# A hybrid decoder block: the second branch's output projection in seven-product quads, halves at both ends, and a new list schedule

## The chip, the cores and the metric

The kernel runs on one core of a Trainium2 chip. The metric is the device time of one execution in microseconds (us); for the kernel before it is the median of three runs. TensorE does the matmuls (PE in the profile, with PEld for its weight loads), VectorE (DVE) and ScalarE (ACT) do the elementwise work, GpSimd (POOL) issues the DMAs that add into what they find, and SyncE (SP) issues the plain loads.

## The reference

One layer, sequence 512, width 1024, fp32; the feed-forward width is 2816 (5632 columns in `w_up`).

```python
h = rmsnorm(x);  p_a, p_b, q, p_g = split(h @ w_in)
gb, gc, v = split(p_a);  y_a = (gb * causal_conv3(gc * v)) @ w_a_out          # branch 0
u, ug = split(p_b)
y_b = silu(layernorm(causal_conv31(u * sigmoid(ug)) + bias)) @ w_b_out         # branch 1
k, vm = split(rmsnorm(mem) @ w_kv)                                             # 256 memory tokens
y_c = attention(q, k, vm, heads=4) @ w_att_out                                 # branch 2
g = sigmoid(p_g + b_gate)
x = x + (g[0] * y_a + g[1] * y_b + g[2] * y_c) @ w_o
gt, up = split(causal_conv3(rmsnorm(x) @ w_up))
x = x + (silu(gt) * up) @ w_down
return rmsnorm(x)
```

## The kernel before

**Precision.** Every operand of a large product is split in two: a high part (`whi`, a rounded copy that ScalarE makes, L444 for weights) and a low part (`wlo`, the difference, by VectorE, L448). A product is then three matmuls: high by high, high by low, low by high. A 128 x 1024 piece of weights that goes through this is a *unit* (`split_job`, `unit_job`); there are four buffers for split units (`UNIT_BUFS`), so the split of a unit can't begin before the unit four places earlier in TensorE's order has been used. With `lo_from` the low part takes another way: ScalarE writes minus the high part (`wn`) and a DMA of POOL's queue adds the weights to it.

**Quads.** The input projection and the up-projection take their 2 x 2 blocks of products with seven block products instead of eight (the Strassen and Winograd scheme). A *quad* covers 1024 rows by 512 columns of weights. `quad_loads` loads four blocks u, v, s, r by SP and makes the sums of weights s5, s6, s7, s3, by accumulating DMAs of POOL or partly by VectorE; seven units come of it, in the order 1, 2, 5, 6, 7, 4, 3 or one close to it. `multiply` (L624) runs one product: 24 matmuls of 256 columns. The other operand stands in seven *forms* with two parts each (`b00`, `b10`, `t5`, `t6`, `t7`, `b11`, `t4`; tiles `fb00h`, `fb00l` and so on), and the three banks a, b, c of a quad are read seven times (`quad_reads`: r1, r5, r6, r4 by ScalarE, r2, r7, r3 by VectorE). 18 quads make the input projection (names in `QUAD_ORDER`: `glu`, `q`, `gate` (branch, half), `cv`, `bb`), 11 the up-projection. `w_o` and the down-projection are seven-product sums too, on larger blocks: `w_o` in the order a, b, f, c, d, e, g, the down-projection as a, b, d, c, f and e, g.

**The branches' output projections.** Each of the three was 8 units of 24 matmuls of 512 columns (`merge_product`, L1349 to L1351): four pairs of output blocks `m`, two halves `g` of the rows. VectorE reads each bank with the branch's gate as a factor (`weigh`), adds branches 2 and 0 (`sum` 0), and adds branch 1 into the tiles `mg` that `w_o` takes as its left operand (`sum` 1). Branch 2's units run after the second gate quad of branch 2, branch 0's after its own gates; branch 1's stand last, directly ahead of `w_o`, as its operand is ready last: the layer norm's scale and `swish`, then a split into `ybh`, `ybl`. `w_o`'s f = m11 - m10 needs all of branch 1; a and b need its first token rows; c, d and e are differences that follow.

**Order.** TensorE's order is written out by hand: `pe()` appends to `seq`, and lists such as `beside` and `first` put other work between the quads' products. The other engines' jobs are placed by a list scheduler (`Jobs`): a job has an engine, an estimated duration, what it follows, buffers that it takes and uses. `latest_starts` works out when each is due at the latest for TensorE; of the jobs that could start next the one with the earliest start, and then the earliest due time, goes first. `LATER` shifts the due times of whole kinds of jobs, `AHEAD` says how far ahead of its due time a kind may start. The result is a fixed queue for each engine (`issue_in_program_order`); an engine waits at an instruction whose operand isn't there, whatever stands behind it. Within a tie the order is that of a Python set. The rows of the input for the residual are loaded late, after `late_rows`.

**The two ends.** At the start TensorE runs nine matmuls on the identity (`warm_up`, L1697), then the first key unit in two halves (`K0`, L818, L822), two value units V 0 0 and V 0 1 (L396), a key unit, another one, and then sums of squares of the memory (`msq`, L734) by a matmul with ones. At the end the down-projection's last sum g runs for row tile 0 and then, as `("pd", "g", "rest")`, 15 matmuls of 512 columns for row tile 1; VectorE adds the bank to the residual (`read`, L1977), ScalarE squares it with a running sum (L1982) and takes the root, VectorE scales the tile (`scaled`, L2004), and it is stored.

## Time and profile before

| | |
|---|---|
| Median of 3 runs | 931.41 us (930.99 to 931.84) |
| The profiled execution | 931.52 us, of it the span 929.3 us |
| TensorE's granted clock in it | 0.997 |
| Busy: TensorE, VectorE, ScalarE | 916.8, 837.3, 672.5 us |
| DMA | 190.59 MB, 205 GB/s on the mean |

The profile's page gives busy times by engine and a line of digits for each, in 40 slices of 23.2 us; the chain that ended last, followed back from the end; and groups of instructions by line and operands. The rows of the timeline that the prediction quotes have a start (us from the start of the span), a duration, the engine, the line, the operation, output and input tiles with their shapes, and how many instructions the row takes together; in brackets stands how long the engine had been idle before, and what released it. A wait that is given by its total names the waiting group, the one that released it, and then total us, times and the longest.

### The profile page before, as it was taken

Reading aid. Unit: us, or ns where it says so; the run is one execution under the profiler, and the core shown is the slowest. Engines: PE = TensorE matmul, PEld = TensorE weight load, DVE = VectorE, ACT = ScalarE, POOL = GpSimd, SP = SyncE. Lnnn points to the kernel's source line nnn. Section 1 sums busy time; section 2 is a strip of 40 time slices with the busy share of each in tenths; the row PEclk is TensorE's granted clock in tenths of the full one; section 3 lists DMA queues with packets and bytes.
Section 4 is the critical chain, followed back from the end, with each engine's and each line's share of the span. In section 5 each row is a group of like instructions: output and inputs, shape, how many; then the busy total and the mean of one; then the engine's idle time right before and its main releaser. Section 6 shows DMA issues by size and latency. Waiting matters only on the chain.

```text
span 929.3 us, 16689 instructions
## 1 busy us (share of the span) xinstructions
PE 916.8 (99%) x6644; PEld 860.5 (93%) x6644; DVE 837.3 (90%) x948; ACT 672.5 (72%) x908; POOL 126.5 (14%) x153
## 2 busy tenths in 40 slices
PE   8999999999999999999999999999999999999996
PEld 7999999999989999999899888898999999988885
DVE  6898999969889999999996778897899889999986
ACT  7676988759978879878856743766767676765655
POOL 0121111101111112110100011021211121002300
PEclk9999999999999999999999999999999999999998
DMA  9999678857676799967955598499999878779962
GB/s 356 371 269 236 137 171 178 201 133 136 170 185 170 177 191 243 210 174 183 226 115 158 186 314 179 97 246 295 258 226 235 209 141 166 195 268 329 251 125 91
DMA packets 54077, 190.59 MB, mean 205 GB/s; under 512 B 6128, under 2 KB 6256, under 8 KB 54000
## 3 DMA queue, kind: packets, MB, share of 16 engines
q0 software_dynamic: 20880, 75.24, 45.5%
q1 hardware_dynamic: 32400, 113.23, 34.0%
q8 instruction: 52, 0.85, 0.4%
q10 hardware_dynamic: 720, 1.06, 0.3%
q14 instruction: 25, 0.20, 0.1%
HBM read 185.31 MB, written 4.19 MB: 204 GB/s over the span
## 4 chain that ended last, share of the span: by engine, by line
PE 93%; DMA 3%; ACT 2%; DVE 1%; issue 1%; SPq 0%; ACTq 0%; POOLq 0%
PE bank L624 56%; PE bank L395 6%; PE bank L397 6%; PE bank L396 6%; PE bank L1349 5%; PE bank L1350 5%; PE bank L1351 5%; DMA wf<-in_w_up 2%; PE bank L871 2%; DMA mem<-in_mem_t 1%; ACT whi L444 0%; DVE wlo L448 0%; PE ss L750 0%; PE bank L1098 0%; ACT j L1982 0%
## 5 line engine op out<-in xcount | busy, mean ns | idle before, releaser
L444 ACT CAST whi<-wf 128x1024 fp32r<-128x1024 f32 (+1 forms) x195 | 202.9, 1044 | 100.9 <-PE bank L624 40.1
L448 DVE TENSOR_TENSOR wlo<-wf,whi 128x1024 fp32r<-128x1024 f32 (+1 forms) x189 | 228.3, 1214 | 29.8 <-ACT whi L444 29.4
L1170 ACT ACTIVATE tp<-u,pk 128x510 f32<-128x510 f32 (+22 forms) x184 | 119.7, 706 | 7.5 <-DVE acc L1177 6.5
L1177 DVE TENSOR_TENSOR acc<-acc,tp 128x1022 f32<-128x1022 f32 (+22 forms) x92 | 109.5, 1193 | 4.2 <-ACT tp L1170 2.4
L582 POOL DMA_DIRECT2D wf<-in_w_in x48 | 42.5, 894 | 229.7 <-DVE wlo L448 164.0
L624 PE MATMUL bank<-ft6h,wlo 128*128 128x256 f32 x232 | 64.4, 278 | 1.2 <-DVE wlo L448 1.2
L624 PE MATMUL bank<-ft6h,whi 128*128 128x256 f32 x232 | 64.6, 278 | 1.0 <-ACT gt L651 1.0
L624 PE MATMUL bank<-fb10h,whi 128*128 128x256 f32 x232 | 64.4, 278 | 0.0
L624 PE MATMUL bank<-fb00h,whi 128*128 128x256 f32 x232 | 64.4, 278 | 0.0
L624 PE MATMUL bank<-fb00l,whi 128*128 128x256 f32 x232 | 64.3, 277 | 0.0
L624 PE MATMUL bank<-fb00h,wlo 128*128 128x256 f32 x232 | 64.3, 277 | 0.0
L624 PE MATMUL bank<-ft7h,whi 128*128 128x256 f32 x232 | 64.3, 277 | 0.0
L624 PE MATMUL bank<-ft7l,whi 128*128 128x256 f32 x232 | 64.3, 277 | 0.0
L624 PE MATMUL bank<-ft7h,wlo 128*128 128x256 f32 x232 | 64.3, 277 | 0.0
L624 PE MATMUL bank<-fb11h,whi 128*128 128x256 f32 x232 | 64.3, 277 | 0.0
L624 PE MATMUL bank<-ft5h,wlo 128*128 128x256 f32 x232 | 64.2, 277 | 0.0
L624 PE MATMUL bank<-ft5h,whi 128*128 128x256 f32 x232 | 64.2, 277 | 0.0
L624 PE MATMUL bank<-ft5l,whi 128*128 128x256 f32 x232 | 64.2, 277 | 0.0
L624 PE MATMUL bank<-ft6l,whi 128*128 128x256 f32 x232 | 64.2, 277 | 0.0
L624 PE MATMUL bank<-fb10h,wlo 128*128 128x256 f32 x232 | 64.2, 277 | 0.0
L624 PE MATMUL bank<-fb10l,whi 128*128 128x256 f32 x232 | 64.2, 277 | 0.0
L624 PE MATMUL bank<-fb11l,whi 128*128 128x256 f32 x232 | 64.1, 276 | 0.0
(392 smaller groups left out, 3143.8 us busy)
## 6 DMA issues: line engine op xcount, KB each, us to landing
wf<-in_w_in SPq DMA_DIRECT2D x52, 512.0 KB, 4.9
wf<-in_w_in POOLq DMA_DIRECT2D x48, 512.0 KB, 5.8
wf<-in_w_up SPq DMA_DIRECT2D x29, 512.0 KB, 5.3
wf<-in_w_up POOLq DMA_DIRECT2D x28, 512.0 KB, 6.9
wf<-in_w_down SPq DMA_DIRECT2D x15, 512.0 KB, 4.2
wf<-in_w_v SPq DMA_DIRECT2D x8, 512.0 KB, 10.1
wf<-in_w_att_out SPq DMA_DIRECT2D x8, 512.0 KB, 3.9
wf<-in_w_a_out SPq DMA_DIRECT2D x8, 512.0 KB, 3.8
```

What stands on the lines that cost most here:

```text
L395: nc.tensor.matmul(ps, s_hi, w_hi, start=start, stop=False, skip_group_check=again)
L396: nc.tensor.matmul(ps, s_hi, w_lo, start=False, stop=False, skip_group_check=again)
L397: nc.tensor.matmul(ps, s_lo, w_hi, start=False, stop=stop, skip_group_check=again)
L444: nc.scalar.copy(parts[0], src())
L448: nc.vector.tensor_tensor(lo, src(), hi.bitcast(F32), op=ALU.subtract)
L582: nc.gpsimd.dma_start(out=tiles[key], in_=block(w, col[c], k), accum_op=ALU.add)
L624: nc.tensor.matmul(ps[:, c, :], w[:, k, at], a[k], start=first and n == 0, stop=i == 3 and n == 2, skip_group_check=again,)
L1170: nc.scalar.activation(two(("tp", p, s))[:, j, s:], two(("u", p))[:, j, : SEQ - s], AF.Copy, scale=weight(j),)
L1177: nc.vector.tensor_tensor(a, a, two(("tp", p, s))[:, :, s:], op=ALU.add)
L1349: nc.tensor.matmul(ps, w_hi[:, i, at], hi, start=first, stop=False)
L1350: nc.tensor.matmul(ps, w_hi[:, i, at], lo, start=False, stop=False)
L1351: nc.tensor.matmul(ps, w_lo[:, i, at], hi, start=False, stop=last)
```

## The change

- **Branch 1.** The eight units become two quads (`("mq", 0)` and `("mq", 1)`), with the products 1, 5, 2, 6, 7, 4, 3 in turn for both. The operand's seven forms are made from the output of `swish` in halves of 512 (`y_parts`), with the sums t5, t7, t6, t4 partly in place. All sums of weights of these quads are DMAs. The reads go to the tile of y, and `weigh` takes y from there; for one quarter of each quad it takes it straight from the bank, with a minus (`weigh_last`, in place of r4).
- **w_o.** The low parts of a and b (four units) come by `lo_from` (`WO_LOWS`). Three units of `w_o` lie in buffers of old forms (`held`) and now wait for the last user of these in `("mq", 1)`. `late_rows` is the first product of `("mq", 1)`.
- **Start.** The first value unit is loaded, split and multiplied in two halves like the first key unit (`halved_unit`); six more matmuls on the identity (`still_warm`) stand between the halves of the key unit; the squares of the memory are put behind the second value unit's high part.
- **End.** The last 15 matmuls become 30 of 256 columns, the left half first; reads and squares of the last row tile go by halves, and `first_end` adds the first half's sum to the rest ahead of the root.
- **Up-projection.** The list `first` of its first products is reordered.
- **Schedule.** `LATER` and `AHEAD` have new entries: 57 and 24 instead of 16 and 8.

```diff
@@ -452,7 +464,7 @@
         def define():
             if held:
                 last = next(f for f in OPERAND if OPERAND[f] == held)
-                before = [(QUAD_ORDER[-1], last)]
+                before = [(("mq", 1), last)]
...
-    def quad_loads(q, w, col0, col1, by_dma=False, take=("wf",), after=()):
+    def quad_loads(q, w, col0, col1, by_dma=False, take=("wf",), after=(), lows=()):
...
+        low = lambda f, c, k: block(w, col[c], k) if f in lows else None
+        split_job((q, 1), u, 4, 256, [("ld", u)], lo_from=low(1, 0, 0))
+        split_job((q, 2), v, 4, 256, [("ld", v)], lo_from=low(2, 0, 1))
...
+        if all_but_4:
+            return
...
-        job(("msq", g), "ACT", actv(1024), mem_square, [("ldm", g, 0), ("ldm", g, 1)],
+        job(("msq", g), "ACT", actv(1024), mem_square,
+            [("ldm", g, 0), ("ldm", g, 1), ("wh", ("V", 0, 1))],
...
+    halved_unit(K0, block(w_kv, 0, 0), 4)
+    halved_unit(V0, w_v[0, 0], 2)
...
+                    still_warm()
...
-    for p in range(4):
-        split_pair(("acc", p), ("ybh", p), ("ybl", p), [("swish", p)])
+    def rows_of(p, r):
+        return two(("acc", p))[:, :, r * HALF : (r + 1) * HALF]
+    def y_parts(key, e, src, after, use):
+        last = next(f for f in OPERAND if OPERAND[f] == key)
+        def pieces(views):
+            if len(views) == 1:
+                return [(slice(0, 2), views[0][:, 2 * e : 2 * e + 2, :])]
+            if e == 0:
+                return [(slice(0, 2), views[0][:, :2, :])]
+            return [(slice(0, 1), views[0][:, 2:3, :]), (slice(1, 2), views[1].unsqueeze(1))]
+        def high():
+            if e == 0:
+                form_tile("y", key)
+            for at, h in pieces(form["y", key, "views"][0]):
+                nc.scalar.copy(h, src()[:, at, :])
+        def low():
+            hi, lo = form["y", key, "views"]
+            for (at, h), (_, l) in zip(pieces(hi), pieces(lo)):
+                nc.vector.tensor_tensor(l, src()[:, at, :], h.bitcast(F32), op=ALU.subtract)
+        hk, lk = ("fh", "y", key, e), ("fl", "y", key, e)
+        job(hk, "ACT", actv(512), high,
+            after + [(("gate", 1, 1), last)] + ([("fh", "y", key, 0)] if e else []), use=use)
+        job(lk, "DVE", dve(512), low, [hk], use=use)
+        form_ready.setdefault(("y", key), []).append(lk)
+        return lk
...
+    Y5 = ("y", "t5")
+    for e in range(2):
+        top, end = ("acc", e), ("acc", 2 + e)
+        done = lambda *ps: [("swish", p) for p in ps]
+        b00 = y_parts("b00", e, lambda e=e: rows_of(e, 0), done(e), [top])
+        b10 = y_parts("b10", e, lambda e=e: rows_of(2 + e, 0), done(2 + e), [end])
+        y_parts("b11", e, lambda e=e: rows_of(2 + e, 1), done(2 + e), [end])
+        t5_half = lambda e=e: four(Y5)[:, 2 * e : 2 * e + 2, :]
+        def y5(e=e, t5_half=t5_half):
+            if e == 0:
+                make(Y5)
+            nc.vector.tensor_tensor(t5_half(), rows_of(e, 0), rows_of(e, 1), op=ALU.subtract)
+        job(Y5 + (e,), "DVE", dve(512), y5, done(e) + ([Y5 + (0,)] if e else []),
+            take=[] if e else [(Y5, ANY)], use=[top] + ([Y5] if e else []))
+        job(("y", "t7", e), "DVE", dve(512), lambda e=e: nc.vector.tensor_tensor(
+            rows_of(e, 1), rows_of(2 + e, 1), rows_of(e, 1), op=ALU.subtract),
+            [Y5 + (e,)] + done(2 + e), use=[top, end])
+        job(("y", "t6", e), "DVE", dve(512),
+            lambda e=e: minus(rows_of(e, 0), rows_of(e, 1), rows_of(e, 0)),
+            [("y", "t7", e), b00], use=[top])
+        job(("y", "t4", e), "DVE", dve(512),
+            lambda e=e: minus(rows_of(2 + e, 0), rows_of(e, 0), rows_of(2 + e, 0)),
+            [("y", "t6", e), b10], use=[top, end])
+        y_parts("t5", e, t5_half, [Y5 + (e,)], [Y5])
+        y_parts("t7", e, lambda e=e: rows_of(e, 1), [("y", "t7", e)], [top])
+        y_parts("t6", e, lambda e=e: rows_of(e, 0), [("y", "t6", e)], [top])
+        y_parts("t4", e, lambda e=e: rows_of(2 + e, 0), [("y", "t4", e)], [end])
...
-            for g in range(2):
-                unit_job(("merge", br, m, g), block(W_OUT[br], m * 256, g), lo_by_dma=br != 1 and 2 < 2 * m + g < 6)
+            for g in range(2) if br != 1 else ():
+                unit_job(("merge", br, m, g), block(W_OUT[br], m * 256, g),
+                         lo_by_dma=2 < 2 * m + g < 6)
...
+                quad = ("mq", m // 2)
+                if m % 2 == 0:
+                    quad_loads(quad, w_b_out, m * 256, m * 256 + 256, by_dma=True, lows=MQ_LOWS)
+                    quad_reads(quad, ("y", m), ("y", m + 1), ANY, all_but_4=True)
+                for r in range(2):
+                    at = slice(r * HALF, (r + 1) * HALF)
+                    held_in = ("y", m)
+                    def weigh(m=m, gate=gate, at=at):
+                        t = two(gate)[:, :, at]
+                        nc.vector.tensor_tensor(t, two(("y", m))[:, :, at], t, op=ALU.mult)
+                    def weigh_last(m=m, gate=gate, at=at, quad=quad):
+                        t = two(gate)[:, :, at]
+                        nc.vector.scalar_tensor_tensor(
+                            t, halves(("bank", quad, "a")), -1.0, t, op0=ALU.mult, op1=ALU.mult)
+                    if m % 2 and not r:
+                        weigh, after, held_in = weigh_last, (quad, 4), ("bank", quad, "a")
+                    else:
+                        after = ("r7", quad) if m % 2 else ("r3" if r else "r2", quad)
+                    job(("weigh", 1, m, r), "DVE", dve(512), weigh, [after, ("sigmoid", 1, m)],
+                        use=[gate, held_in])
...
-    late_rows = [("merge", 1, 0, 1)]
+    late_rows = [(("mq", 1), 1)]
...
+    WO_LOWS = [(p, i) for p in "ab" for i in range(2)]
...
+                      lo_from=WO_SRC[p][i] if (p, i) in WO_LOWS else None)
...
+    still_warm = lambda: pe(("warm", 1), 0.7, lambda: warm_up(6), use=[("bank", "warm")], unit=False)
...
-        (GATE[1, 1], 3): lambda: [pe_merge(1, m) for m in range(4)],
+        (GATE[1, 1], 3): lambda: [
+            multiply_job(("mq", q), f, "y") for f in (1, 5, 2, 6, 7, 4, 3) for q in range(2)],
...
+    ENDS = [slice(0, 256), slice(256, 512)]
...
-            pe(("pd", "g", "rest"), 5 * 3 * MM, lambda: steps("g", (3, 4, 5), (1,)),
-               use=banks + [(s, p, g) for s in ("zh", "zl") for g in (1, 2)], unit=False)
...
+            for i, cols in enumerate(ENDS):
+                pe(("pd", "g", "rest", i), 15 * MM_QUAD,
+                   lambda cols=cols: steps("g", (3, 4, 5), (1,), cols),
+                   use=banks + [(s, p, g) for s in ("zh", "zl") for g in (1, 2)], unit=False)
...
-    first = [(UP[0], 1), (UP[0], 2), "tr2", (UP[1], 1), "tr3", (UP[1], 2), (UP[2], 1), (UP[0], 5), (UP[2], 2), (UP[0], 6), (UP[1], 5), (UP[0], 7), (UP[0], 3), (UP[0], 4), (UP[1], 6), (UP[2], 5), (UP[1], 7), (UP[2], 6), (UP[1], 4), (UP[1], 3)]
+    first = [(UP[0], 1), (UP[0], 2), "tr2", (UP[1], 1), "tr3", (UP[1], 2), (UP[2], 1), (UP[0], 5), (UP[1], 5), (UP[0], 6), (UP[2], 2), (UP[0], 7), (UP[1], 6), (UP[0], 4), (UP[0], 3), (UP[1], 7), (UP[2], 5), (UP[1], 4), (UP[1], 3)]
...
+    def first_end():
+        ss = ss_fin[NT - 1][:, 1:2]
+        nc.vector.scalar_tensor_tensor(ss, ss_end, 1.0 / D, ss, op0=ALU.mult, op1=ALU.add)
...
+                for i, end in enumerate(ENDS):
+                    job(("rd", p, t, i), "DVE", dve(256), lambda end=end: read("g", 1, end),
+                        [("pd", "g", "rest", i)] + rows_in, use=[("bank", chain(p), t)])
...
+            job(("sr", t, 0), "ACT", 0.4, lambda: square(last, 0, ENDS[0], ss_end),
+                [("rd", "g", 1, 0)])
+            job("ends", "DVE", 0.1, first_end, [("sr", t, 0), ("hd", t)])
+            job(("sr", t, 1), "ACT", 0.4, lambda: square(last, 0, ENDS[1]), [("rd", "g", 1, 1)])
+            ready = [("sr", t, 1), "ends"]
```

166 lines of the change are left out of this document (91 added, 75 removed), and 17 rows, old and new, of tables (AHEAD, LATER).

## The prediction

> **What bounds the kernel now.** I read the page first, then TensorE's waits, then the timeline of the stages that the change touches.
>
> ```profile
> span 929.3 us, 16689 instructions
> PE 916.8 (99%) x6644; PEld 860.5 (93%) x6644; DVE 837.3 (90%) x948; ACT 672.5 (72%) x908; POOL 126.5 (14%) x153
> ...
> DVE  6898999969889999999996778897899889999986
> ...
> PEclk9999999999999999999999999999999999999998
> ...
> PE 93%; DMA 3%; ACT 2%; DVE 1%; issue 1%; SPq 0%; ACTq 0%; POOLq 0%
> ```
>
> TensorE is busy for 916.8 of 929.3 us at a full granted clock, and 93% of the chain is its work. VectorE is close behind: 90%, with its only loose stretch in slices 21 to 25 (488 to 604 us), where the changed projection lies. The waits of TensorE say how little a better order alone could win (engine, line, releaser: total us, times, longest):
>
> ```profile
> PE bank L624 <- DVE wlo L448: 1.2, 2, 0.8
> PE bank L624 <- ACT gt L651: 1.0, 2, 0.8
> PE bank L396 <- DVE wlo L448: 0.8, 1, 0.8
> PE bank L871 <- ACT whi L818: 0.5, 1, 0.5
> PE bank L871 <- DVE wlo L822: 0.2, 1, 0.2
> ```
>
> The two of L624 (2.2 us) are in the first products of the up-projection, the three others (1.5 us) in the first 11 us. Nothing else stands still between the first product and the last. So the change must win by fewer column passes, by the two ends, or not at all; and whatever keeps TensorE waiting is lost in full.
>
> **Products.** Branch 1's projection is 8 units of 24 matmuls of 512 columns, 192 in all; after, 2 quads of 7 products of 24 matmuls of 256 columns, 336. The prices are the distance from the first of the 192 to the first matmul of w_o, and a stretch of the chain that is all quad products:
>
> ```profile
> 516.63 0.39 PE L1349 MATMUL bank<-ybh,whi 128*128 128x512 f32 x1
> 560.17 0.39 PE L395 MATMUL bank<-whoh,mgh 128*128 128x512 f32 x1
> ...
> 287.66 153.12 PE bank L624 x1344
> ```
>
> 43.54 us / 192 = 226.8 ns; 153.12 / 1344 = 113.9 ns. The stage falls from 43.54 to 336 x 0.1139 = 38.28: **-5.26 us**, all of it on the path. A rule that speaks against narrow matmuls is in the Trainium skill, "TensorE: Matmul & The Clock Gate", Part 1: a warm matmul takes N / 2.4 GHz plus some 2.5 ns each, so two halves cost more than a whole. By it the term would be 192 x 215.8 ns - 336 x 109.2 ns = -4.8 us. The rows show no such part: 2 x 113.9 = 227.8 against 226.8. I keep -5.26.
>
> **Start.** The stretch from the first product to the fourth unit, by TensorE, ScalarE and VectorE:
>
> ```profile
> 1.36 4.21 PE L1697 MATMUL bank<-ident 128*128 128x128 f32 x18 [1.36 <-POOL ident masks.py:199]
> 5.24 0.58 PE L871 MATMUL bank<-mh,whi 128*128 128x256 f32 x1
> ...
> 6.24 0.28 PE L871 MATMUL bank<-mh,whi 128*128 128x256 f32 x1
> ...
> 7.17 0.28 PE L871 MATMUL bank<-mh,wlo 128*128 128x256 f32 x1
> ...
> 8.66 0.39 PE L871 MATMUL bank<-mh,wlo 128*128 128x256 f32 x1 [0.23 <-DVE wlo L822]
> ...
> 11.09 0.50 PE L396 MATMUL bank<-wlo,mh 128*128 128x512 f32 x1 [0.77 <-DVE wlo L448]
> ...
> 16.47 0.28 PE L871 MATMUL bank<-mh,whi 128*128 128x256 f32 x1
> ...
> 7.27 0.60 ACT L818 CAST whi<-wf 128x512 fp32r<-128x512 f32 x1
> 7.78 1.05 ACT L734 ACTIVATE msq<-mem 128x1024 f32<-128x1024 f32 x1
> ...
> 7.91 0.69 DVE L822 TENSOR_TENSOR wlo<-wf,whi 128x512 fp32r<-128x512 f32 x1
> 9.81 3.50 DVE L448 TENSOR_TENSOR wlo<-wf,whi 128x1024 fp32r<-128x1024 f32 x3 [1.21 <-ACT whi L444]
> ```
>
> The first key unit's second half can't run before its low part is done (8.66). The six new matmuls on the identity fill the gap behind the first half: at half of the 234 ns that 18 passes took cold, 12 passes are 1.4 us, from 7.28 to 8.69; that costs nothing beyond 0.03. The second half then runs closed up: 12 x 0.114, to 10.06. Now ScalarE squares the memory (7.78) ahead of the value unit, and TensorE waits for its low part until 11.09. After, the squares stand behind the second value unit's high part, and the value unit comes in halves: high 7.78 to 8.38, low to about 9.2, the second halves 0.6 later, all ahead of 10.06. The two value units end at 10.06 + 24 x 0.2268 = 15.50 instead of 16.47: **-0.97**. Should the identity matmuls run at the cold pace (2.8 us) the gain is nothing; this is the bad end. The next wait is the sum of squares of the memory, which is wanted 5.5 us later (one value unit's successor K 1 0 and K 0 1, 2.73 each); two squares and a sum are some 3.3 us, so it is covered.
>
> **End.** The last row of tokens:
>
> ```profile
> 921.53 0.39 PE L397 MATMUL bank<-whi,zl 128*128 128x512 f32 x1
> ...
> 922.02 0.75 DVE L2004 SCALAR_TENSOR_TENSOR x<-x,cols,gfin 128x512 f32<-128x512 f32 x1
> 922.69 0.68 DVE L1977 TENSOR_TENSOR x<-x,bank 128x512 f32<-128x512 f32 x1
> 924.68 0.75 DVE L2004 SCALAR_TENSOR_TENSOR x<-x,cols,gfin 128x512 f32<-128x512 f32 x1
> ```
>
> The last read starts 0.77 late because VectorE scales the tile before (922.02). After, the last 15 matmuls are 30 of half the width, the first half's read and square lie under the second half, and only a read and a square of 256 columns remain: about 0.3 less for the read and 0.2 for the square; the earlier read of tile 2 lets the scaling before it go 0.35 sooner. **-0.85**, between -0.3 (the two short ones alone, and the new small addition in front of the root) and -1.2.
>
> **VectorE between the projections.** Here the change costs. VectorE in the stage, from branch 1's first product to the first matmul of w_o's third combination f, which needs everything of branch 1 (columns: us, then busy and count of PE, PEld, DVE, ACT, POOL, clock, DMA share, GB/s), and its spacing for 1024, 512 and 512 from a bank:
>
> ```profile
> 502.00:516.60 14.60, 14.60 (x103) 13.55 (x102) 12.40 (x13) 12.35 (x15) 0.00 (x0) 1.00 0.24 74
> 516.60:571.10 54.50, 54.50 (x241) 44.88 (x240) 41.78 (x47) 29.03 (x34) 5.17 (x6) 1.00 0.85 257
> ...
> 506.00 4.61 DVE L1261 TENSOR_TENSOR acc<-acc,rows 128x1024 f32<-128x1024 f32 x4
> 530.07 1.29 DVE L1400 TENSOR_TENSOR mg<-g,g 128x512 f32<-128x512 f32 x2
> 527.73 1.29 DVE L1382 TENSOR_TENSOR g<-bank,g 128x512 f32<-128x512 f32 x2 [1.14 <-PE bank L1351]
> ...
> 519.58 1.28 ACT L1373 ACT_TABLE_LOAD   x1
> ...
> 568.04 1.22 DVE L740 TENSOR_TENSOR wo<-wo,wo 128x1024 f32<-128x1024 f32 x1
> 569.18 1.22 DVE L1505 TENSOR_TENSOR mgl<-mg,mgh 128x1024 fp32r<-128x1024 f32 x1
> ...
> L624 PEld LDWEIGHTS bank<-fb00h,whi 128*128 128x128 f32 x232 | 43.6, 188 | 0.1
> ```
>
> (The last row, TensorE's weight loads by shape, serves a rival below.) Instructions follow each other more closely than they last: 568.04 to 569.18 is 1.13 us for 1024, and in the same way 0.61 and 0.64 for the other two. Before, VectorE has 12.7 us to spare in these 54.5. After, the time shrinks to 38.28 + 10.9 = 49.2, and the work grows: 6 more weight lows (+6.8), 16 half forms and differences that come after the first product (+9.8), 6 reads of banks (+3.9), against 2 lows of the old operands (-2.3) and 4 lows of w_o that go to ScalarE and a DMA (-4.5): +13.7. That is 55.5 in 49.2; some 3.5 of it (like the difference of weights for c at 568.04, and first row sums) can wait, so **about 3 us are missing** even without a gap. The queue as built says the same: the low part of product (1, 2) can't start until product (1, 1) has freed its buffer and ScalarE has made the high part, 6.5 us into the stage; from there to f's low part VectorE has 20 of 1024, 28 of 512, 2 of 256 and 11 from banks, 22.6 + 17.1 + 0.7 + 7.0 = 47.4 us, in 42.7: 4.7 missing. The planner leaves ties to the order of a Python set, and the queue differs from build to build: in the mildest order f's low part comes in time, and weight lows behind it miss by 2.1; in the harshest 50.4 us stand ahead of it, 7.3 too much. A wait on ScalarE comes on top: its queue has a table load (1.28) and gates ahead of the high part of (1, 6), +1.3. So TensorE stands still in w_o for 2.1 to 8.6 us; I take **+4.0**, between the mild order with its wait (3.4) and the one of the file as built (4.7). Products of the quads themselves are in time by 0.6 us or more (the low parts of b11 ahead of f = 3 are the closest).
>
> **DMA.** The mixed window above has a share of 0.85 at 257 GB/s. The queues:
>
> ```profile
> q0 software_dynamic: 20880, 75.24, 45.5%
> q1 hardware_dynamic: 32400, 113.23, 34.0%
> ```
>
> A 512 KB addition by POOL takes 0.455 x 929.3 / 143.5 = 2.9 us of all engines, a load 1.5. The change adds 12 additions (35 us), 8 for the quads and 4 for w_o's lows; about half fall behind the first product. They fit only because rows and later weights can wait. POOL's queue is in order, so w_o's additions stand behind s3, and b's low lands close to when it is wanted (46 us into the stage). I cost this at nothing, because VectorE is late at nearly the same place; alone it is 0 to 5.
>
> **First up-products.** The order of the list is changed around the 2.2 us of waits, but (1, 6) follows (1, 5) after three products instead of four, and the add and two splits between them are 2.9 plus about 2.3. I take 0, from -2.2 (the waits go) to +2.2 (as much again). The rest of the schedule shows no engine overfilled: 0.
>
> **Sum.** The profiled execution took 931.52 us (span 929.3 and 2.2 around it; the median of the runs is 931.41). 931.52 - 5.26 - 0.97 - 0.85 + 4.0 = **928.4 us**.
>
> **Rivals.** (1) Everything is hidden: VectorE does weighing and sums late enough that f is in time, and one of the up-waits goes: 931.52 - 7.08 = 924.4, down to 923.4. For it: work of 3.5 us that can wait. Against: a queue that is full by sum. (2) The harsh order, slower: f's low part 8.6 late, in one piece, and TensorE restarts cold. From the start rows a cold restart loses 0.66 (three distances in 1.00 us, 5.24 to 6.24, instead of 0.34): 931.52 - 7.08 + 8.6 + 0.66 = 933.7. It decides the sign from 7.1 us of standstill on. The same page of the Trainium skill (its table of the clock gate) halves the clock after an idle window of about 3.4 us and for as long again, which would be 1.7 us instead of 0.66. No run here shows it; no wait above is longer than 0.8. (3) w_o's lows land late by DMA on top of VectorE: standstill 6.5, 930.9. For it: share 0.85 already. (4) Matmuls of 256 columns don't reach their pace with new weights each time: 336 x 188 ns of weight load would be 63 us. Against it are the 1344 above.
>
> **Chances.** Forecast 0.45 (own range 926.5 to 930), (1) 0.20, (2) 0.20, (3) 0.14, (4) 0.01. A difference of 0.2% (1.9 us) is about what can be told here. Faster by more: most of the forecast and (1), 0.60; within: a part of the forecast and of (3), 0.20; slower: (2) with ends of (3) and (4), 0.20. The range 924.2 to 933.9 leaves out part of (1), below, and part of (2), above, with (4).
>
> **What would show it.** TensorE's waits: L841 and L871's first waits gone, the third key unit near 15.5; the 336 matmuls at 113.9 ns; new waits on lows of w_o (f, c) by DVE, 2 to 9 us, VectorE without idle from 7 us into the stage. It is wrong if w_o runs closed up, if the waits name a DMA, or if products of the quads wait.

## The result: 0.4% slower, and the profile after

The changed kernel takes 935.32 us (median of 8 runs, 933.39 to 936.70) against 931.51 (8 runs, 930.99 to 933.26): a ratio of 1.0038, 95% interval 1.0026 to 1.0050. The forecast was 928.4, range 924.2 to 933.9. The profiled execution took 936.52 us (span 934.8), 5.0 more than that of before; it is one of the slower of the eight, so its account below is some 1.2 us longer than the medians' difference of 3.8. The page of the changed kernel begins so:

```profile
span 934.8 us, 17114 instructions
PE 917.3 (98%) x6815; PEld 867.9 (93%) x6815; DVE 848.7 (91%) x978; ACT 684.5 (73%) x938; POOL 137.1 (15%) x165
...
PEclk9999999999999999999999998999999999999998
...
PE 90%; DVE 4%; DMA 2%; ACT 1%; issue 1%; ACTq 0%; DVEq 0%
```

TensorE is busy for as long as before (917.3 us against 916.8), although the change took 5 us of column passes away, and the line of its clock has an 8 in slice 25 (561 to 584 us, w_o) that it didn't have. VectorE is now 4% of the chain that ended last. TensorE's waits in the changed kernel (engine, line, releaser: total us, times, longest):

```profile
PE bank L407 <- ACT mgh L1624: 3.1, 1, 3.1
...
PE bank L409 <- DVE mgl L1629: 1.1, 1, 1.1
PE bank L637 <- ACT gt L664: 1.1, 1, 1.1
```

The two upper ones are new. Both are the first product of w_o's f, once for the high and once for the low part of m11 - m10. The third, in the first up-products, is not new: before, TensorE waited there for the same tile, 1.0 us in two waits. TensorE's timeline gives the stages their lengths:

```profile
15.57 0.28 PE L893 MATMUL bank<-mh,whi 128*128 128x256 f32 x1
...
515.74 0.28 PE L637 MATMUL bank<-fb00h,whi 128*128 128x256 f32 x1
...
554.27 0.39 PE L407 MATMUL bank<-whoh,mgh 128*128 128x512 f32 x1
...
926.05 0.28 PE L409 MATMUL bank<-whi,zl 128*128 128x256 f32 x1
```

The third key unit, branch 1, w_o and the last matmul start at these times. With the first up-product (600.81 us before, 602.71 after) and the first matmul of the down-projection (808.49 and 812.76) the account is:

| stage | before, us | after, us | difference | forecast |
|---|---|---|---|---|
| up to the third key unit | 16.47 | 15.57 | -0.90 | -0.97 |
| from there to branch 1 | 500.16 | 500.17 | 0.0 | 0 |
| branch 1, to the first of w_o | 43.54 | 38.53 | -5.01 | -5.26 |
| w_o and transposes, to the first up-product | 40.64 | 48.44 | +7.80 | +4.0 |
| up-projection, to the first of the down-projection | 207.68 | 210.05 | +2.37 | 0 |
| down-projection to the last matmul | 113.04 | 113.29 | +0.25 | in the next |
| from the last matmul to the end of the span | 7.77 | 8.75 | +0.98 | -0.85 |

The differences add up to 5.5 us, the growth of the span; the execution grew by 5.0, as the time outside the span fell from 2.2 to 1.7 us.

What TensorE does in w_o ahead of f and behind it, and the two rows by which f's high part is released (VectorE's difference m11 - m10, then ScalarE's rounded copy of it):

```profile
565.23 0.40 PE L409 MATMUL bank<-whoh,mgl 128*128 128x512 f32 x1
568.77 0.80 PE L407 MATMUL bank<-whi,mgh 128*128 128x512 f32 x1 [3.14 <-ACT mgh L1624]
569.36 0.63 PE L408 MATMUL bank<-wlo,mgh 128*128 128x512 f32 x1
571.10 0.80 PE L409 MATMUL bank<-whi,mgl 128*128 128x512 f32 x1 [1.10 <-DVE mgl L1629]
571.69 0.63 PE L407 MATMUL bank<-whi,mgh 128*128 128x512 f32 x1
...
574.68 0.54 PE L408 MATMUL bank<-wlo,mgh 128*128 128x512 f32 x1
575.06 0.39 PE L409 MATMUL bank<-whi,mgl 128*128 128x512 f32 x1
...
566.42 1.22 DVE L1607 TENSOR_TENSOR mg<-mg,mg 128x1024 f32<-128x1024 f32 x1
...
567.67 1.04 ACT L1624 CAST mgh<-mg 128x1024 fp32r<-128x1024 f32 x1 [0.27 <-DVE mg L1607]
```

From 565.23 to 568.77 stand 3.31 us of idle time (the matmul's own place of 0.23 taken off). From 569.36 to 571.10 another 1.51, for the low part: 4.8 us idle (the two waits' own figures, 3.1 and 1.1, count from the modelled end of the matmul before). From 549 us on VectorE works without a wait up to f's difference (566.42), so f is late because that difference comes late in VectorE's queue. The other matmuls from 568.77 to 575.06 are slow: 0.59 us instead of 0.23 for the first, 3.96 instead of 2.04 for the nine from 571.10 on, 2.3 us more. That is 7.1 of the 7.8 us (0.3 of the rest are a and b, whose matmuls follow each other at 0.233). Matmuls of 0.43 instead of 0.23 us mean a clock at a half, which the rows by stretch (length, then busy time and count of PE, PEld, DVE, ACT and POOL, clock, DMA share, GB/s) show here and once more behind two waits in the up-projection (the last two rows, from the timeline, are these waits):

```profile
568.70:575.10 6.40, 5.23 (x12) 3.69 (x13) 6.40 (x8) 1.68 (x3) 1.75 (x2) 0.51 0.94 278
575.10:580.00 4.90, 4.90 (x23) 4.06 (x22) 4.90 (x6) 2.43 (x3) 0.86 (x1) 1.00 1.06 329
...
654.90:660.40 5.50, 5.02 (x27) 4.82 (x28) 5.50 (x7) 4.32 (x7) 2.01 (x3) 0.69 1.05 319
...
654.90 0.38 PE L637 MATMUL bank<-ft6h,whi 128*128 128x256 f32 x1 [1.06 <-ACT gt L664]
...
655.88 0.39 PE L637 MATMUL bank<-ft6h,wlo 128*128 128x256 f32 x1 [0.48 <-DVE wlo L460]
```

The clock is 0.51 in the first row. The third has 16 distances of 0.21 us instead of 0.11 (656.91 to 660.31), 1.6 us more; the other 0.7 of the up-projection's 2.37 are waits, 3.7 us against 2.9 before (both with the matmuls' own places taken off).

VectorE over branch 1 and over w_o, before and after, two rows each:

```profile
516.63:560.17 43.54, 43.54 (x195) 36.06 (x193) 31.05 (x34) 25.21 (x30) 3.45 (x4) 1.00 0.84 263
560.17:600.81 40.64, 40.64 (x186) 33.17 (x184) 37.15 (x44) 21.54 (x29) 4.22 (x5) 1.00 0.58 139
```

```profile
515.74:554.27 38.53, 38.53 (x338) 38.40 (x337) 35.20 (x46) 33.71 (x47) 7.80 (x9) 1.00 1.03 258
554.27:602.71 48.44, 43.75 (x186) 34.54 (x185) 45.97 (x58) 25.82 (x35) 6.93 (x8) 0.93 0.93 251
```

Its work grows from 68.2 to 81.2 us. TensorE's, closed up, is 38.5 + 40.6 = 79.1 us. So in these two stages VectorE has become the longer of the two, 2 us over even if it never waited. It does wait, 5.8 us in all, and longest here (ScalarE's row, then VectorE's):

```profile
545.57 1.05 ACT L456 CAST whoh<-wf 128x1024 fp32r<-128x1024 f32 x1 [3.99 <-DMA wf<-in_w_o]
...
549.07 1.22 DVE L460 TENSOR_TENSOR wlo<-wf,whi 128x1024 fp32r<-128x1024 f32 x1 [2.05 <-ACT whi L456]
```

ScalarE stands for 4 us at the high part of a w_o unit whose load is late, and a weight's high part that VectorE wants is queued behind it.

The end (the last matmul was at 926.05):

```profile
926.37 0.42 DVE L2111 TENSOR_TENSOR x<-x,bank 128x256 f32<-128x256 f32 x1 [2.04 <-PE bank L409]
926.71 0.16 DVE L2144 RECIPROCAL cols<-cols 128x1 f32<-128x1 f32 x1
926.90 0.75 DVE L2146 SCALAR_TENSOR_TENSOR x<-x,cols,gfin 128x512 f32<-128x512 f32 x1
928.61 0.16 DVE L2135 SCALAR_TENSOR_TENSOR cols<-cols 128x1 f32<-128x1 f32 x1 [0.95 <-ACT j L2117]
928.68 0.41 DVE L2111 TENSOR_TENSOR x<-x,bank 128x256 f32<-128x256 f32 x1
```

The read of the first half waits until the second half is done too, and the second half's read stands behind the new small addition (928.61), which waits for ScalarE's square. Nothing of the halves overlaps.

### The profile page after: what moved, and what is told of

It is laid out like the page before. It is cut to its first block, busy times and chain, and to the rows that moved or that the text cites. A ratio compares the mean times of both kernels' runs of the same rounds, so it can differ in the third digit from the quotient of the medians.

```text
span 934.8 us, 17114 instructions
## 1 busy us (share of the span) xinstructions
PE 917.3 (98%) x6815; PEld 867.9 (93%) x6815; DVE 848.7 (91%) x978; ACT 684.5 (73%) x938; POOL 137.1 (15%) x165
## 3 DMA queue, kind: packets, MB, share of 16 engines
q10 hardware_dynamic: 720, 1.06, 0.3%
## 4 chain that ended last, share of the span: by engine, by line
PE 90%; DVE 4%; DMA 2%; ACT 1%; issue 1%; ACTq 0%; DVEq 0%
PE bank L637 59%; PE bank L409 6%; PE bank L407 6%; PE bank L408 6%; PE bank L1444 3%; PE bank L1446 3%; PE bank L1445 3%; PE bank L893 2%; DMA wf<-in_w_up 2%; DVE wlo L460 1%; PE ss L766 0%; ACT whi L456 0%; PE bank L1132 0%; DVE mg L1519 0%; DMA pk<-in_packed 0%
## 5 line engine op out<-in xcount | busy, mean ns | idle before, releaser
L456 ACT CAST whi<-wf 128x1024 fp32r<-128x1024 f32 (+1 forms) x201 | 209.3, 1043 | 99.9 <-PE bank L637 34.8
L460 DVE TENSOR_TENSOR wlo<-wf,whi 128x1024 fp32r<-128x1024 f32 (+1 forms) x195 | 235.4, 1212 | 31.4 <-ACT whi L456 30.9
L1204 ACT ACTIVATE tp<-u,pk 128x511 f32<-128x511 f32 (+22 forms) x184 | 119.2, 704 | 7.3 <-DVE acc L1211 6.3
L1211 DVE TENSOR_TENSOR acc<-acc,tp 128x1022 f32<-128x1022 f32 (+19 forms) x92 | 109.1, 1188 | 6.2 <-ACT tp L1204 5.1
L637 PE MATMUL bank<-ft6h,whi 128*128 128x256 f32 x248 | 69.4, 280 | 1.1 <-ACT gt L664 1.1
L637 PE MATMUL bank<-ft6h,wlo 128*128 128x256 f32 x248 | 69.5, 280 | 0.5 <-DVE wlo L460 0.5
L637 PE MATMUL bank<-ft6l,whi 128*128 128x256 f32 x248 | 69.4, 280 | 0.0
L637 PE MATMUL bank<-ft5l,whi 128*128 128x256 f32 x248 | 68.9, 278 | 0.4 <-DVE ft5l L562 0.4
L637 PE MATMUL bank<-ft5h,whi 128*128 128x256 f32 x248 | 68.8, 278 | 0.0
L637 PE MATMUL bank<-ft7h,whi 128*128 128x256 f32 x248 | 68.8, 277 | 0.0
```

What stands on the lines that cost most here:

```text
L456: nc.scalar.copy(parts[0], src())
L460: nc.vector.tensor_tensor(lo, src(), hi.bitcast(F32), op=ALU.subtract)
L637: nc.tensor.matmul(ps[:, c, :], w[:, k, at], a[k], start=first and n == 0, stop=i == 3 and n == 2, skip_group_check=again,)
L1204: nc.scalar.activation(two(("tp", p, s))[:, j, s:], two(("u", p))[:, j, : SEQ - s], AF.Copy, scale=weight(j),)
L1211: nc.vector.tensor_tensor(a, a, two(("tp", p, s))[:, :, s:], op=ALU.add)
```

## The experiments

Two theories of the standstill at f after the result: (A) VectorE's volume of work in branch 1 and w_o keeps f waiting; (B) late loads and the order of the queues do. Two more beside them: idle time of TensorE halves its clock, and the end's first read waits for the whole bank. Each trial has an A and a B of its own, given in its expectation. Since the planner breaks ties by the order of a set, all kernels from here on have one line changed.

**Fixed ties.**

```diff
-            for k in set(users.get(key, ())):
+            for k in dict.fromkeys(users.get(key, ())):
```

> The changed kernel with one line of the planner altered: ties are broken in the order of definition instead of a set's order, so that every build has the same queues; it is the base of the experiments that follow. All theories expect the changed kernel's time within its spread, 933.4 to 936.7 us, with the same three losses in the trace: w_o some 46 to 49 us from its first matmul to the first up-product (40.6 before), the first up-products 1 to 3 us slower than before, and the end from the last matmul on about 1 us longer than before. If w_o is back at 41 to 43, the loss lay in the order of that one build and not in the change.

935.36 us (932.86 to 937.26, 6 runs), ratio 1.0035 [1.0019, 1.0052]. The trace has the same three losses: w_o 48.80, up-projection 209.98, end 8.71. The loss isn't that of one build. One build spreads over 4.4 us, so effects of 1 to 2 us are read from the stages of the profile first. These vary too: w_o takes 48.44 us in the changed kernel, 48.80 here and 50.00 in the next trial, which alters the end alone.

**The end's halves in banks of their own.** The bank with the earlier sum is read ahead of them, which is one more read of 512 columns.

```diff
+                end = ("bank", "end", i)
                 pe(("pd", "g", "rest", i), 15 * MM_QUAD,
-                   lambda cols=cols: steps("g", (3, 4, 5), (1,), cols),
+                   lambda cols=cols, end=end: steps("g", (3, 4, 5), (1,), cols, end),
+                   take=[(end, "ps")], ...
```

> Fixed ties, and the last row tile's two halves go to two banks of their own; the bank with the earlier sum is read ahead of them (one more read of 512, beside TensorE's work). Theory A (the first half's read waits for the second half because both lie in one bank tile): the first read of 256 starts some 1.5 us ahead of TensorE's last matmul instead of behind it, the span from the last matmul to the end falls from about 8.7 to about 7.0 us, and the kernel is 1.5 to 2.0 us faster than with fixed ties alone. Theory B (the end is late for the queues of ScalarE and VectorE, with scaling of tile 2 ahead): the first read comes earlier but the end moves by less than 0.5 us.

VectorE in this kernel (TensorE's last matmul is at 926.25):

```profile
925.05 0.41 DVE L2116 TENSOR_TENSOR x<-x,bank 128x256 f32<-128x256 f32 x1
...
926.35 0.75 DVE L2156 SCALAR_TENSOR_TENSOR x<-x,cols,gfin 128x512 f32<-128x512 f32 x1
927.02 0.41 DVE L2116 TENSOR_TENSOR x<-x,bank 128x256 f32<-128x256 f32 x1
```

The first read is now ahead of the last matmul, and the end takes 7.25 us instead of 8.71: theory A in the trace. The median hardly moved (935.27, 934.17 to 935.32, 5 runs, ratio 1.0033 [1.0020, 1.0046]), against the 1.5 to 2.0 us expected; in this profile w_o's 1.2 us more stand against the gain. Beside the other remedy, below, the median with own banks is 1.1 us lower than without (933.17 and 932.05; the intervals of the ratios overlap a little). The scaling of tile 2 at 926.35 still stands ahead of the second read.

**TensorE kept busy ahead of f; then also inside f.** In w_o, 12 matmuls on the identity between b and f; in the second kernel 6 more between f's second and third matmul.

```diff
+            if p == "f" and i == 0:
+                gap_warm()
             pe_wo(p, i)
```

> Fixed ties, and 12 matmuls on the identity (24 passes of 128 columns, about 2.5 us at the pace of the start) between w_o's b and f, where TensorE waits for VectorE. Theory A (after the standstill of 3 us the clock falls to a half, and the first matmuls of f take 0.43 us each instead of 0.23): no half-clock stretch behind the gap, f's matmuls at 0.23 from the start, and 1.5 to 2.5 us faster than with fixed ties alone; f still starts as late. Theory B (the slow matmuls there wait for their operands, or the clock falls for another reason): the same slow stretch, and the time is the same or up to 1 us longer.

> Fixed ties; 12 matmuls on the identity ahead of w_o's f as in the first such trial, and 6 more between f's second and third matmul, where f waits for its low part: TensorE is nearly never idle there. In the first trial f's low part came 1.76 us late and eight matmuls behind it still took 0.43 us. Theory A (idle time of TensorE alone brings the half clock): no stretch of slow matmuls in w_o, f starts as late as before, and w_o takes 46.5 to 47.3 us (48.8 with fixed ties alone, 48.5 with the first gap filled). Theory B (another cause): the slow stretch stays, and w_o takes 48 us or more.

Clock in the stretch behind f's first matmuls with the first gap filled, then in w_o's middle with both:

```profile
569.00:571.20 2.20, 0.73 (x2) 0.30 (x2) 2.20 (x4) 0.67 (x1) 0.00 (x0) 1.00 0.99 266
571.20:575.60 4.40, 4.27 (x12) 3.42 (x13) 4.40 (x6) 1.26 (x2) 1.75 (x2) 0.63 1.03 293
```

```profile
560.00:580.00 20.00, 19.28 (x102) 16.21 (x101) 20.00 (x23) 7.14 (x7) 3.48 (x4) 1.00 1.02 331
```

With one gap filled TensorE still waited 0.67 us ahead of f and 1.60 for its low part (1.5 us idle from 569 to 571.2), the clock still fell, to 0.63, and w_o took 48.48 us: the slow stretch that A of this trial excluded. With both filled the clock stays at 1.00, f starts at 568.67 (568.99 with fixed ties alone), and w_o takes 46.99: theory A for the clock, worth 1.8 us in the profile (0.3 of it the earlier start), and 1.5 to 3.0 against the three values above. Times: 933.85 (930.67 to 934.71, 10 runs, ratio 1.0019 [1.0008, 1.0031]) and 933.17 us (932.04 to 935.65, 10 runs, 1.0020 [1.0009, 1.0032]). The medians are 1.5 and 2.2 us below fixed ties, with intervals that overlap, so the medians alone don't show the gain. The first kernel's, at an unchanged w_o, is in its profile one of the up-projection: 207.15 us, without a slow stretch.

**The first up-products in the old order.**

```diff
-    first = [..., (UP[0], 5), (UP[1], 5), (UP[0], 6), (UP[2], 2), (UP[0], 7), (UP[1], 6), ...]
+    first = [..., (UP[0], 5), (UP[2], 2), (UP[0], 6), (UP[1], 5), (UP[0], 7), (UP[0], 3), ...]
```

> Fixed ties, and the order of the first up-products as before the change. Theory A (the new order of the list loses the 2.4 us at the start of the up-projection, by closer dependent products and a half-clock stretch behind them): the distance from the first up-product to the first of the down-projection falls from 210 to about 207.7, and the kernel is 1.5 to 2.5 us faster than with fixed ties alone. Theory B (the loss comes from late transfers and VectorE's lateness carried over from w_o, whatever the order): the distance stays within 0.7 us of that with fixed ties.

940.07 us (ratio 1.0089 [1.0074, 1.0104]): the up-projection takes 212.68 us, with one wait of 3.3 us and 26 matmuls at half clock. Both theories fell. The new order is the better one here. What it loses against before is mostly the slow stretch, and that comes and goes among kernels with this order: 210.0 us with it (fixed ties), 208.1, 207.2 and 206.6 without it (own banks, first gap, both gaps). The waits alone don't decide it: two of 1.06 and 0.48 us brought it in the changed kernel, and two of 1.25 and 0.48 at the same place in the kernel with four low parts fewer (next trial) didn't:

```profile
650.80:653.30 2.50, 0.77 (x5) 0.56 (x5) 2.50 (x3) 2.50 (x4) 0.00 (x0) 1.00 1.04 272
653.30:658.00 4.70, 4.70 (x42) 4.64 (x42) 4.70 (x6) 4.61 (x8) 2.45 (x4) 1.00 1.06 335
```

What decides is open.

**Fewer low parts: products 4 and 3, then also 6 and 7.** These products take the weights' high part in place of the low one, so that VectorE does four or eight instructions of 1024 less. These kernels leave out the weights' low parts in those products, and with them the precision, so only their times are of use.

```diff
+            if unit[0] in (("mq", 0), ("mq", 1)) and unit[1] in (4, 3):
+                job(("wl", unit), "NONE", 0.0, lambda: None, [("wh", unit)], use=use)
+            elif lo_from is None:
```

> Fixed ties, and products 3 and 4 of both branch-1 quads take the high part of the weights in place of the low one; these four low parts (4 x 1.13 = 4.5 us of VectorE) are left out, everything else stays. With fixed ties alone f's first matmul starts 3.5 us late and its low part is another 1.5 us late. Theory A (VectorE has more work than time ahead of f): standstill at f falls from 5 to below 1 us, the half-clock stretch goes with it, w_o takes 41 to 42.5 us instead of 48.8. Theory B (late loads: ScalarE stands 3.6 us at the high part of a w_o unit whose load is late, and VectorE behind it 2.3): VectorE's work is gone but the wait stays, f is late by 2 us or more, and w_o takes 45 us or more.

> Fixed ties; products 6, 7, 4 and 3 of both branch-1 quads take the high part of the weights in place of the low one, and these eight low parts (9.0 us of VectorE) are left out. VectorE's work in branch 1 and w_o together falls from 81.2 to about 72.2 us, where TensorE's matmuls closed up take 78.9. Theory A (volume): the standstill at f goes but for 1 us, the two stages take 79 to 81.5 us instead of 87.4. Theory B (late loads of w_o hold ScalarE, and VectorE behind it, whatever the volume): f is late by 2 us or more as with four low parts fewer, and the two stages take 83 us or more.

With four fewer, w_o takes 46.28 us and f's high and low part are 1.46 and 1.76 late; the two stages take 84.7 us. That is what B expected (45 or more, f late by 2 us or more) and not A (41 to 42.5, below 1): VectorE still waits for ScalarE behind the late load, 2.7 us in this trace. With eight fewer (the rows begin 0.2 us ahead of branch 1):

```profile
515.85:554.25 38.40, 38.40 (x340) 38.40 (x339) 33.00 (x49) 36.88 (x51) 8.69 (x10) 1.00 1.04 262
554.25:596.76 42.51, 40.94 (x186) 33.11 (x185) 38.75 (x46) 22.51 (x29) 6.07 (x7) 1.00 0.95 272
```

VectorE has 71.6 us, the two stages take 80.7 (87.4 with fixed ties alone), f waits 1.1, and the clock stays up. The w_o loads were not touched, and a load that ends as late (545.6) holds ScalarE for 0.7 us and VectorE not at all: theory A. The queues are others than with fixed ties, too, so the trial doesn't separate the volume from the order altogether. The kernels as wholes took 933.78 us (1.0025 [1.0012, 1.0038]) and 940.15 (1.0094 [1.0078, 1.0110]); in the second one the planner's queue makes an up-product wait 5.0 us for its operand, and two slow stretches follow (up-projection 216.96).

**w_o's adding DMAs left out; more of them for the quads.**

```diff
-    WO_LOWS = [(p, i) for p in "ab" for i in range(2)]
+    WO_LOWS = []
```

```diff
-    MQ_LOWS = ()
+    MQ_LOWS = (1, 2)
```

> Fixed ties, and the low parts of w_o's a and b are made by VectorE again (4 x 1.13 us more for it, four additions by DMA of 512 KB and four copies of ScalarE fewer). Theory A (VectorE's volume): standstill in w_o grows by 3 to 4.5 us, w_o takes 51 to 54 us, the kernel is 3 to 5 us slower than with fixed ties alone. Theory B (late loads and crowded DMA): the loads of w_o land earlier, and w_o takes as long as with fixed ties or less (45 to 49).

> Fixed ties, and the low parts of products 1 and 2 of both branch-1 quads come by ScalarE and an adding DMA (4.5 us less for VectorE, 3.9 more for ScalarE, four more DMAs of 512 KB, some 12 us of all DMA engines). Theory A (VectorE's volume): standstill at f falls by 3 us or more, w_o takes 42 to 45 us. Theory B (late loads and crowded DMA): loads land later still, ScalarE stands longer, w_o takes 48 us or more, or products of the quads themselves begin to wait.

Without w_o's additions the two stages take 97.0 us (VectorE 86.7), and the kernel 945.70 (1.0150 [1.0135, 1.0166]): the sign of A at twice its size (it expected 3 to 5 us more, B none): a low part of b's operand comes 7.9 us late from VectorE's queue. With four more additions the quads' own products wait, 7.2 us for additions by DMA and 11.2 for a high part of ScalarE behind them, and the kernel takes 953.64 us (1.0236 [1.0221, 1.0251]); w_o itself then runs in 42.4, behind a branch 1 of 63.3. A's sign for w_o and B's for the quads both came, so this run doesn't tell them apart. Four additions fewer and four more both lost: with the transfers' share at 1.03 in branch 1 already, no more of VectorE's load went to DMA at this place.

**w_o's loads in another ring; and this with four low parts fewer.**

```diff
-            ("a", w_o[0, i], "wf"), ("b", w_o[0, 2 + i], "wf"), ("y", ...
+            ("a", w_o[0, i], "lf"), ("b", w_o[0, 2 + i], "lf"), ("y", ...
```

> Fixed ties, and the weights of w_o's a and b are loaded into another ring of buffers (lf) as soon as the gate quads are through, so that they don't wait for one of the six load buffers. VectorE's work is unchanged. Theory A (VectorE's volume alone): ScalarE's wait for the load goes, f is late by as much as before within 0.7 us, w_o 48 to 49. Theory B (late loads): VectorE's idle 2.3 us and ScalarE's 3.6 go, f's standstill falls from 5 to about 2.7, the half-clock stretch shrinks or goes, w_o 44 to 46.5. Both in part: between these.

> Fixed ties; four low parts left out (products 4 and 3; 4.5 us of VectorE, work 76.7 us), and w_o's a and b loaded early into the other ring. Four low parts fewer gave 84.7 us for the two stages with the load late. Theory A (volume alone): about the same, 84 to 85.5, or the wait moves to the norm as it did with early loads. Theory B (late loads alone): 82 or less already with this volume. Both (work below TensorE's time, and loads in time, are needed): 79.5 to 82.5, less than either alone, with neither f nor the norm late by over 1 us.

TensorE's waits with the loads apart:

```profile
PE bank L1710 <- DVE cols L1701: 3.0, 1, 3.0
...
PE bank L407 <- DVE x L1684: 2.2, 1, 2.2
...
PE bank L409 <- DVE mgl L1629: 0.6, 1, 0.6
```

f is nearly in time (0.6), as B had it, but VectorE still has its 81.2 us: the reads of banks come 2.2 late and the norm ahead of the transposes 3.0, and w_o takes 49.98 us, no less than without the remedy (937.54 us, 1.0061 [1.0046, 1.0076]). The wait moved. With four low parts fewer as well all three expectations (A, B, both) fell: the two stages take 86.7 us, as this build's b waits 5.6 us for its low part by DMA (936.18 us, 1.0040 [1.0026, 1.0054]).

**Work moved off VectorE.** Branch 1's eight sums on GpSimd; then f's low part ahead of c's difference, with d's low parts by DMA.

```diff
-                        nc.vector.tensor_tensor(
+                        nc.gpsimd.tensor_tensor(
...
-                    job(("sum", 1, m, r), "DVE", dve(512), merged,
+                    job(("sum", 1, m, r), "POOL", 1.0, merged,
```

```diff
-    WO_LOWS = [(p, i) for p in "ab" for i in range(2)]
+    WO_LOWS = [(p, i) for p in "abd" for i in range(2)]
-    minus_job(("ms", "c"), m10, m00, m00, [("ms", "f")] + ...
+    minus_job(("ms", "c"), m10, m00, m00, [("ms", "f"), ("mgl", "f")] + ...
```

> Fixed ties, and the eight sums of branch 1 into w_o's operand (128 x 512 each, 4.8 us of VectorE) are made by GpSimd. Over branch 1 and w_o together VectorE has 81.2 us of work; TensorE's matmuls, closed up, take 78.9 there. Theory A (VectorE's volume in the two stages): its work falls to 76.4 us, below TensorE's, and the two stages take 82 to 85 us instead of 87.4 (84.2 before). Theory B (the order of the queues and late loads, not the volume): they take 86.5 us or more. GpSimd's sums may be slow (no row of its elementwise work is known here) or stand behind its DMAs; if one takes over 2 us, f is late by their chain, and then this run can't tell.

> Fixed ties; VectorE makes f's low part ahead of the difference for c, and the low parts of w_o's d come by ScalarE and an adding DMA instead of VectorE (2.3 us less for it, behind branch 1's loads). Theory A (VectorE's volume): 81.2 falls to 78.9 us, f's first matmul 1 to 2.3 us earlier and its low part 2 to 3 us earlier, the two stages take 84 to 86 us instead of 87.4, if c doesn't wait for d's additions. Theory B (crowded DMA): c or d waits for its weights by 1 us or more, and the two stages take 87 us or more.

The first can't tell A from B, as its expectation allowed. GpSimd needs 1.5 to 1.6 us a sum (VectorE 0.60) and its DMAs queue behind them; f's last four sums end at 575.3, and the kernel takes 949.54 us (1.0199 [1.0178, 1.0220]):

```profile
568.87 6.43 POOL L1519 TENSOR_TENSOR mg<-g,g 128x512 f32<-128x512 f32 x4 [10.17 <-PE bank L408]
```

The second came out as B had it. VectorE's work fell to 78.8 us, as A wanted, but the two stages take 87.0 us (A: 84 to 86, B: 87 or more): w_o's f and c wait for their weights (ScalarE's high parts 3.4 us, low parts 1.5), f's behind a load that lands at 570.1, while f's operand is ready by 564.2, and the up-projection takes 214.6 us (942.24, 1.0121 [1.0100, 1.0142]).

Over all these trials neither theory suffices. Less work for VectorE shortens the stages (eight low parts fewer) and more lengthens them (w_o's additions left out); but late loads still hold f with 4 or 2 us of work less (four fewer, low part first), and early loads alone move the wait.

**Start and end alone, in the kernel before.** The parts of the diff for the two ends, the end in banks of its own, and nothing else.

> The kernel before (ties fixed), with only the new start (first value unit in halves, six matmuls on the identity, later squares of the memory) and the new end, its halves in banks of their own; branch 1, the tables and the first up-products are those of before. By the traces so far: third key unit at 15.55 instead of 16.47 (-0.9), w_o and the up-projection as before, the 30 narrow matmuls and the last one's place +0.3, the end 7.25 instead of 7.77 (-0.5): 1.1 us faster than before, 930.3. Rival: the planner's other queues that follow from the new start cost it again, 931 to 933.

The profile does what was expected (third key unit 15.62, w_o 40.72, end 7.29, span 928.1 against 929.3), but the median is that of before, 931.69 us, ratio 1.0000 [0.9991, 1.0010], and not the 930.3 expected. The profiled run was the fastest of its ten (930.28). No version here beats the kernel before by what can be measured.

**Both gaps filled and the end in its own banks.** The two diffs above together, in the changed kernel.

> Fixed ties, both gaps in w_o filled with matmuls on the identity, and the two halves of the last row tile in banks of their own. If the two remedies add up (no slow stretch -2.2 in the median, end -1.5): 931.2 to 932.2, and in the profile w_o 47, end 7.25. What is left against 928.4 would then be the standstill of 6 instead of 4 and the 30 narrow matmuls.

932.05 us (930.82 to 934.38, 12 runs), ratio 1.0004 [0.9995, 1.0013]: w_o 47.15, end 7.28, as expected. Its profiled run was the slowest of the twelve; the up-projection took 210.19 us in it, with one wait of 2.8 and a slow stretch behind it. With the clock in w_o and the end mended the change is worth nothing measurable, instead of the 3.1 us that were forecast.

## Why the prediction was wrong

The terms forecast -3.1 us, and the span grew by 5.5: 8.6 us too much in the profile (6.9 in the medians). Of these, w_o has 3.8, the up-projection 2.4 and the end 2.1. **The step that failed most is one that the sum left out: the half clock behind a standstill,** 2.3 us in w_o and 1.6 in the up-projection, nearly half of the miss. The second is the overlap at the end, the third the size of VectorE's term.

**Products, start: right.** -5.01 for -5.26 (38.53 / 336 = 114.7 ns for 113.9), and -0.90 for -0.97; the twelve passes on the identity took 1.26 us for 1.4.

**VectorE between the projections: the standstill about right, the term too small.** It was +7.80 for +4.0. Of the miss of 3.8, idle time makes 0.8, the clock 2.3, and 0.7 is small change. The idle time was 4.8 us, 3.3 for the high and 1.5 for the low part of f's operand, and VectorE's lateness at f is what the prediction named. That 4.0 came so near is in part luck: it was taken between 3.4 for the mild order, which holds ScalarE's wait of 1.3, and 4.7 for the queue as built, which doesn't; with it that is 6.0. (The harshest order's 50.4 us in 42.7 are 7.7 too much, not 7.3; the upper end was 9.0.) Of the signs, c's low part never waited, and VectorE was not without idle time: it waited 2.05 us behind a late load. Nor could the 3.5 us that were let "wait" be made up in w_o, which is nearly as full (37.15 of 40.64 us before): the run with the loads apart shows them late again at the reads and the norm. Over both stages the prediction's own rows give 68.2 + 13.7 = 81.9 us of VectorE (measured 81.2) in 38.3 + 40.6 = 78.9, 3.0 too much, which is less than the term's 4.0.

**The clock: in no term.** A cold restart was priced at 0.66 us, and that only in the second rival. It cost 2.3 us in w_o by the rows above and 1.8 by the trial (46.99 against 48.80 with the gaps filled). The rows of before had no such case, as no wait in them was longer than 0.8 us.

The Trainium skill, "TensorE: Matmul & The Clock Gate", Part 1, has the clock at a half after an idle window of about 3.4 us, and the estimate of 1.7 us from it stood beside the rival. The length agrees: the slow stretch in the up-projection lasts 3.4 us (656.91 to 660.31), that in w_o 6.3 (568.77 to 575.06). The condition doesn't: no wait of 3.4 us was needed, as 0.67 and 1.60 us with two matmuls between them were enough with the first gap filled, and 1.06 and 0.48 us in the up-projection.

**First up-products: taken as 0, measured +2.37.** The bound of +2.2 was nearly it, but for another reason. The waits changed little (+0.7); the rest, 1.6, is the half clock. Without it kernels with the new order take 206.6 to 208.2 us for 207.68.

**End: -0.85, measured +1.23 with the narrow matmuls.** The step "the first half's read and square lie under the second half" failed: both halves write one bank tile, and the read waits for the last write to it. Own banks gave 1.5 us back. The 30 matmuls cost 0.12 us each, not 0.114, in one bank and in two.

**DMA: "nothing, because VectorE is late at nearly the same place"** held in part. With 9 us less for VectorE a load that ends as late harms nobody; but with 4.5 less, or with f's low part first, late loads keep the stages long. That b's low part by DMA can be next showed with early loads and four low parts fewer (5.6 us late).

**The rivals.** The second, slower by a harsh order and a cold clock, gave 933.7 for 935.3. Its mechanism is the nearest, but that its figure is near is luck: it had 8.6 us in one piece and 0.66 for the clock; measured were 4.8 in two pieces and 2.3 for the clock in w_o, 1.6 for the clock in the up-projection, and 2.1 more than forecast at the end. The first (all hidden) had no room. With the clock in w_o and the end mended, 932.05 us remain 3.6 above the forecast; no run takes these apart further.

## What to carry to other kernels

Price a new standstill of TensorE with the clock behind it: here waits of 4.8 us cost 2.3 more, and waits of 1.5 us in the up-projection 1.6 more. Price an overlap within one tile at nothing until the trace shows the second instruction starting early. When TensorE's time is cut, sum up the other engines' work over the whole stretch until they are next idle: what is put off ahead of one product came up late at the next. The sum says whether a standstill can be hidden, not how long it is. And count what operand forms cost: here seven forms for only two quads saved 5.0 us of TensorE and cost VectorE 13.

## What the runs showed of the hardware

Two waits of 0.67 and 1.60 us with two matmuls between them were followed by eight matmuls at half clock, 3.4 us long; with 12 and 6 matmuls on the identity in the gaps the clock stayed at 1.00. Short waits brought a slow stretch in some kernels and not in others: 1.06 and 0.48 us did in the changed kernel, 1.25 and 0.48 didn't with four low parts fewer, 0.70 and 0.76 in w_o didn't in the trial with f's low part first. The spread of one build's times is not explained by this: with fixed ties the granted clock falls from 0.995 at 932.86 us to 0.992 at 937.26, but the changed kernel's eight runs are all at 0.992 or 0.993 and spread by 3.3 us. A sum of 128 x 512 took GpSimd 1.5 to 1.6 us where VectorE takes 0.60.
